# Two-layer hybrid trunk on one core: the first two weight steps multiplied unsplit

## The chip, the core and the metric

The kernel runs on one core of a Trainium2 chip. The metric is the device time of one execution in microseconds; the kernel before was timed three times, and the median is what the changed kernel is compared with.

Five engines work side by side, each through its own queue in program order: TensorE (PE: matmuls; its weight loads are listed as PEld), VectorE (DVE), ScalarE (ACT), GpSimdE (POOL) and SyncE (SP, which issues the loads). Results are handed on by semaphores.

## What is computed

A trunk of two layers over 256 tokens of width 2048, in fp32. Layer 0 is a chunked gated linear attention, layer 1 a spatial-gating MLP; each has an RMS norm ahead of it and one behind it. Cut to what matters here:

```
def reference(x, norm_pre, ..., gla_w_in, ..., sgu_w_out):
    for i in range(2):
        h = rmsnorm(x, norm_pre[i])
        y = gla_mixer(h, ...) if i == 0 else sgu_mixer(h, ...)
        x = x + rmsnorm(y, norm_post[i])
    return x

def gla_mixer(h, w_in, ...):
    proj = h @ w_in                      # (256 x 2048) @ (2048 x 6160)
    q, k, v, g, glr = jnp.split(proj, ...)
    ...
    return o @ w_out
```

The time goes into four large projections (146 MB of weights pass through once). The change concerns only the first columns of the first one: the first 512 columns of q.

## The kernel before

**Tiles.** The 256 tokens are two tiles of 128 (t = 0, 1). A projection is worked off in column groups of 512 columns, a group in eight steps (`NS`) of two K tiles of 128 rows (`KC`); one step's weights are a tile `raw` of 128 x 2 x 512, loaded by L98. Steps are numbered through the whole program: 0 to 7 are the first group, 8 to 15 the second.

**Products in three parts.** An fp32 product is made of three float32r ones. Weights are split by `split` (L105): ACT rounds `raw` to `whi` (L110), DVE or POOL takes the difference `wlo` (L111). The operand is split in the same way by `split_T` (L201): ACT writes `hTh` (L205), DVE `hTl` (L206). PE then multiplies hTh by whi, hTl by whi and hTh by wlo (L178, L179, L180). Step 0 alone is loaded and split in halves of one K tile.

**The operand of layer 0.** `make_hT(t, c)` (L280) makes four K tiles (chunk c of 4) of token tile t: four PE transposes of x (L211), a DVE multiplication by the norm's gain into `ttmp` (L284), and `split_T`. Chunk c serves steps 2c and 2c + 1, and again the same steps of all later groups of the layer.

**What sets the order.** Everything is issued in the order in which the code is run; there is no scheduler. `Stream.run` (L188) walks over the parts (step i, token tile t). In the first group two steps take turns: (0,0) (1,0) (0,1) (1,1), (2,0) (3,0) (2,1) (3,1), and so on. In the middle of a part, behind its first three products, `mid` may run a `make_hT` (L762 to L766). Behind a part, L196 fetches (loads and splits) the steps up to 2 ahead in the first group, up to 4 ahead later. With `START`, the `wlo` of steps 0, 2, 4 and 6 are POOL's; the others are DVE's. When the last step of the first group is issued, `q_done` (L295) puts the row norm on the queues: four sums of squares on ACT (`sq`, L229), two small DVE operations, one of POOL, and the scaling of the result on DVE (`q`, L301).

**The start.** Loads of x come in eight pieces of 256 KB (`load_x`), each weight step is 512 KB; L768 to L773 set their order. `WARM` transposes of the identity run on PE until the first piece of x is there, `FILL` more stand behind the first transposes of x.

Of the kernel before, what the change touches and what calls it, by code (L numbers as in the profile page):

```python
# [13 lines left out]
PSUM = bass.MemoryType.PSUM  # L14
# [10 lines left out]
AHEAD = 4  # L25
WARM = 14
FILL = 6
POOL = (1, 3, 5)
START = (0, 2, 4, 6)
SLOTS = 24  # L30
# [5 lines left out]
def trunk(  # L36
# [52 lines left out]

# [1 line left out]
    def load(parts, c, fine):  # L91
# [24 lines left out]
    class Stream:  # L116
        """Projections, column group by column group, in steps of KC K tiles; both tiles of
        tokens use a step's weights. What follows a group's products is a generator, whose
        stages come one by one between the parts that follow; a stage may ask for more parts
        before the next. Around a boundary (a group whose operand is the end of all groups  # L120
        before it) the tiles of tokens take turns of LAG steps, so that each one's products
        cover what the other waits for."""

        def __init__(self, groups, boundaries, mid):
            self.mid = mid
            self.groups = groups
            self.steps = [(g, c) for g in range(len(groups)) for c in range(NS)]
            self.raw, self.split, self.ps, self.live = {}, {}, {}, []
            n = len(self.steps)
            self.order = []  # L130
            i = 0
            turns = {b * NS + d: LAG for b in boundaries for d in (-LAG, 0)}
            turns.update({d: 2 for d in range(0, NS, 2)})
            self.pool_lo = set(START) | {b * NS + d for b in boundaries for d in POOL}
            while i < n:
                m = turns.get(i, 1)
                self.order += [(i + d, t) for t in range(NT) for d in range(m)]
                i += m

        def load(self, i):  # L140
            if i < len(self.steps) and i not in self.raw:
                g, c = self.steps[i]
                self.raw[i] = load(self.groups[g]["parts"], c, i == 0)

        def fetch(self, i):
            if i < len(self.steps) and i not in self.split:
                self.load(i)
                eng = nc.gpsimd if i in self.pool_lo else nc.vector
                self.split[i] = split(self.raw[i], eng, i == 0)

# [14 lines left out]
        def part(self, i, t):  # L165
            g, c = self.steps[i]
            grp = self.groups[g]
            w = sum(n for _, _, n in grp["parts"])
            if c == 0:
                self.ps[g, t] = acc.tile([P, 512], F32, name="acc", tag="acc")  # L170
            pt = self.ps[g, t][:, :w]
            ah, al = grp["lhs"]()
            sl = slice(t * P, (t + 1) * P)
            wh, wl = self.split[i]
            for k in range(KC):
                kt = c * KC + k
                xh, xl = ah[kt // 4][:, kt % 4, sl], al[kt // 4][:, kt % 4, sl]
                nc.tensor.matmul(pt, xh, wh[:, k, :], start=kt == 0, stop=False)  # L178
                nc.tensor.matmul(pt, xl, wh[:, k, :], start=False, stop=False)  # L179
                nc.tensor.matmul(pt, xh, wl[:, k, :], start=False, stop=kt == KT - 1)  # L180
                if k == 0 and (i, t) in self.mid:
                    self.mid[i, t]()
            if t == 0 and c == 2 and "pre" in grp:
                self.start(grp["pre"]())
            if c == NS - 1:
                self.start(grp["done"](t, pt))

        def run(self):  # L188
            freed, at = 0, 0
            for i, t in self.order:  # L190
                self.part(i, t)
                self.advance()
                if t == NT - 1:
                    freed = i + 1
                at = max(at, i)
                for j in range(at + 1, min(at + (AHEAD if at >= NS else 2), freed + SPLITS - 1) + 1):  # L196
                    self.fetch(j)
            while self.live:
                self.advance()

# [46 lines left out]

# [1 line left out]
    xs = [const.tile([P, D], F32, name=f"x{t}", tag=f"x{t}") for t in range(NT)]  # L249
# [26 lines left out]

# [281 lines left out]

# [1 line left out]
    def out_groups(key, w_out, gain, name, end, extra=None):  # L560
# [86 lines left out]

# [1 line left out]
    W2 = sgu_w_in[0]  # L649
# [110 lines left out]

# [1 line left out]
    mid = {(0, 0): lambda: make_hT(1, 0), (1, 0): lambda: make_hT(0, 1)}  # L762
    for c in range(1, 4):
        mid[2 * c - 1, 1] = lambda c=c: make_hT(1, c)
        if c < 3:
            mid[2 * c + 1, 0] = lambda c=c: make_hT(0, c + 1)  # L766
    s = Stream(groups, [layer1, len(groups)], mid)
    for c in range(4):  # L768
        load_x(0, c)
        if c < 2:  # L770
            s.load(2 * c)
            s.load(2 * c + 1)
        load_x(1, c)  # L773
    warm = aux.tile([P, 4, P], F32, name="warm", tag="aux")
# [4 lines left out]
    nc.vector.tensor_copy(gpre0, vps[:, 0:KT])  # L779
    s.fetch(0)  # L780
    make_hT(0, 0)
    for i in range(FILL):
        nc.tensor.transpose(warm[:, i % 4, :], ident, ident)
    s.fetch(1)
    s.run()
# [32 lines left out]
```

## Time and profile before

| | |
|---|---|
| median of three runs | 774.06 us (773.51 to 775.16) |
| span of the profiled execution, first to last instruction | 772.0 us |
| PE busy | 755.7 us, 98% of the span |
| DVE, ACT, POOL busy | 452.9, 353.7, 87.6 us |
| DMA | 146.28 MB, mean 189 GB/s over the span |

The profiled execution has no time of its own beside its span; the median of the timed runs is 2.06 us above the span, which is what lies around it. PE is busy nearly throughout, so the profile is read where PE is not busy or is slow: at the start, and at the boundary between the layers. The views used are the timeline (instructions in order of time, with the idle time ahead of each on its engine and what ended it), the stretches (busy time and granted TensorE clock of one microsecond each), and the chain that ended last.

### The profile page before, as it was taken

The numbers are of one execution on the slowest core, as the hardware profiler recorded it, in microseconds if no ns is written. First come the engines' busy times: TensorE is split into PE (matmuls) and PEld (weight loads), VectorE is DVE, ScalarE is ACT, GpSimd is POOL, SyncE is SP. The second block draws the span as 40 slices with busy tenths as digits, with TensorE's granted clock in tenths as the row PEclk, the third lists the DMA queues.
The fourth block names the chain that finished last, engine by engine and source line by source line (L and its number), as shares of the span: only waits on it lengthen the run. The fifth ranks groups of instructions, "written<-read, shape, count | busy, mean of one in ns | idle before, by whom it ended". The sixth has DMA issues, their size and how long they took to land.

```text
span 772.0 us, 9465 instructions
## 1 busy us (share of the span) xinstructions
PE 755.7 (98%) x3560; PEld 633.4 (82%) x3560; DVE 452.9 (59%) x521; ACT 353.7 (46%) x473; POOL 87.6 (11%) x81
## 2 busy tenths in 40 slices
PE   8999999999999999999989999999999999999995
PEld 6889998888888888888867888888888888888884
DVE  4666764645465545766588564555556565565443
ACT  4654753534354434444446454444335445344430
POOL 3210010000000001403041000132232000000000
PEclk9999999999999999999999999999999999999998
DMA  9576583465755567664724855666766455656633
GB/s 302 162 209 186 159 259 110 136 218 165 216 166 168 169 196 232 215 219 167 264 88 137 272 190 192 196 208 215 227 217 203 152 166 169 195 182 234 203 104 110
DMA packets 81318, 146.28 MB, mean 189 GB/s; under 512 B 7196, under 2 KB 14900, under 8 KB 81272
## 3 DMA queue, kind: packets, MB, share of 16 engines
q1 hardware_dynamic: 81240, 145.66, 59.5%
q8 instruction: 28, 0.46, 0.2%
q14 instruction: 18, 0.15, 0.1%
q10 hardware_dynamic: 32, 0.01, 0.0%
HBM read 143.55 MB, written 2.10 MB: 189 GB/s over the span
## 4 chain that ended last, share of the span: by engine, by line
PE 94%; DVE 2%; issue 1%; DMA 1%; ACT 0%; SPq 0%; POOLq 0%; POOL 0%; DVEq 0%; ACTq 0%
PE acc L180 30%; PE acc L178 30%; PE acc L179 30%; PE tp L211 2%; PE op L519 1%; DVE hp L614 1%; DMA raw<-in_gla_w_in_dram 1%; PE sc L440 1%; PE sp L371 0%; PE sc L433 0%; DVE h2l L206 0%; DVE wlo L111 0%; DVE x L752 0%; DVE x L590 0%; PE sc L446 0%
## 5 line engine op out<-in xcount | busy, mean ns | idle before, releaser
L111 DVE TENSOR_TENSOR wlo<-raw,whi 128x1024 fp32r<-128x1024 f32 (+2 forms) x257 | 316.6, 1254 | 119.6 <-ACT whi L110 119.2
L110 ACT CAST whi<-raw 128x1024 fp32r<-128x1024 f32 (+3 forms) x265 | 264.7, 1021 | 141.7 <-PE acc L179 57.5
L178 PE MATMUL acc<-whi,hTh 128*128 128x512 f32 (+2 forms) x416 | 158.7, 382 | 1.4 <-ACT hTh L205 1.4
L179 PE MATMUL acc<-whi,hTl 128*128 128x512 f32 (+2 forms) x416 | 155.9, 375 | 0.2 <-DVE hTl L206 0.2
L180 PE MATMUL acc<-wlo,hTh 128*128 128x512 f32 (+2 forms) x416 | 156.0, 375 | 0.0
L178 PE MATMUL acc<-whi,h2h 128*128 128x512 f32 x384 | 151.5, 394 | 0.0
L179 PE MATMUL acc<-whi,h2l 128*128 128x512 f32 x384 | 150.0, 391 | 0.0
L180 PE MATMUL acc<-wlo,h2h 128*128 128x512 f32 x384 | 149.8, 390 | 0.0
L178 PEld LDWEIGHTS acc<-whi,hTh 128*128 128x128 f32 x416 | 78.5, 189 | 13.3 <-ACT hTh L205 1.7
L180 PEld LDWEIGHTS acc<-wlo,hTh 128*128 128x128 f32 x416 | 78.4, 189 | 12.9
L179 PEld LDWEIGHTS acc<-whi,hTl 128*128 128x128 f32 x416 | 78.6, 189 | 12.7 <-DVE hTl L206 0.6
L180 PEld LDWEIGHTS acc<-wlo,h2h 128*128 128x128 f32 x384 | 72.4, 188 | 15.3
L178 PEld LDWEIGHTS acc<-whi,h2h 128*128 128x128 f32 x384 | 72.4, 189 | 14.4
L179 PEld LDWEIGHTS acc<-whi,h2l 128*128 128x128 f32 x384 | 72.4, 189 | 14.3
L178 PE MATMUL acc<-whi,ogTh 128*128 128x512 f32 x128 | 50.2, 392 | 0.0
L178 PE MATMUL acc<-whi,tTh 128*128 128x512 f32 x128 | 50.0, 391 | 0.0
L179 PE MATMUL acc<-whi,tTl 128*128 128x512 f32 x128 | 49.8, 389 | 0.0
L180 PE MATMUL acc<-wlo,ogTh 128*128 128x512 f32 x128 | 49.8, 389 | 0.0
L180 PE MATMUL acc<-wlo,tTh 128*128 128x512 f32 x128 | 49.8, 389 | 0.0
L179 PE MATMUL acc<-whi,ogTl 128*128 128x512 f32 x128 | 49.8, 389 | 0.0
L703 POOL TENSOR_TENSOR vg<-vg,gb 128x512 f32<-128x512 f32 x16 | 27.8, 1735 | 61.4 <-DVE vg L701 41.1
L229 ACT ACTIVATE sq<-acc 128x512 bf16<-128x512 f32 x16 | 9.5, 596 | 50.3 <-PE acc L180 50.3
(155 smaller groups left out, 586.9 us busy)
## 6 DMA issues: line engine op xcount, KB each, us to landing
raw<-in_sgu_w_in_dram SPq DMA_DIRECT2D x96, 512.0 KB, 4.8
raw<-in_gla_w_in_dram SPq DMA_DIRECT2D x79, 512.0 KB, 4.6
raw<-in_gla_w_out_dram SPq DMA_DIRECT2D x32, 512.0 KB, 5.7
raw<-in_sgu_w_out_dram SPq DMA_DIRECT2D x32, 512.0 KB, 4.8
raw<-in_gla_w_in_dram SPq DMA_DIRECT2D x16, 344.0 KB, 3.7
raw<-in_gla_w_in_dram SPq DMA_DIRECT2D x8, 336.0 KB, 3.6
x<-in_x_dram SPq DMA_DIRECT2D x8, 256.0 KB, 7.4
gb<-in_norm_post_dram SPq DMA_DIRECT2D x8, 256.0 KB, 6.2
```

Source lines behind the costliest of these rows:

```text
L110: nc.scalar.copy(hi[:, ks], raw[:, ks])
L111: eng.tensor_tensor(lo[:, ks], raw[:, ks], hi[:, ks].bitcast(F32), op=ALU.subtract)
L178: nc.tensor.matmul(pt, xh, wh[:, k, :], start=kt == 0, stop=False)
L179: nc.tensor.matmul(pt, xl, wh[:, k, :], start=False, stop=False)
L180: nc.tensor.matmul(pt, xh, wl[:, k, :], start=False, stop=kt == KT - 1)
L211: nc.tensor.transpose(tp[:, k, :], src[:, k * P : (k + 1) * P], ident)
L229: nc.scalar.activation(sq[:, : src.shape[1]], src, AF.Square, accum_out=dst)
L440: nc.tensor.matmul(sc[:, o + C : o + P], k2[c][:, i, o : o + P], qT[c][:, i, o + C : o + P], start=jl == 0, stop=jl == JH - 1,)
L519: nc.tensor.matmul(op, a, b, start=i == 0, stop=i == len(ops) - 1)
L614: nc.vector.scalar_tensor_tensor(hp[c], yp[c][:, t, :], r, xp[c][:, t, :], op0=ALU.mult, op1=ALU.add)
L703: nc.gpsimd.tensor_tensor(a, a, st["lng"][:, i, :], op=op)
```

## The change

Steps 0 and 1 (`WHOLE = 2`) are not split. PE multiplies `raw` itself, as fp32, by `ttmp` itself, one product in place of three; `ttmp` of chunk 0 is kept, and its `split_T`, which later groups need, is moved to the end of the first group: for t = 0 into part (7,0), for t = 1 into part (6,1). Steps 0, 1 and 2 are loaded in halves, and step 2 is split in halves. The `make_hT` of the first chunks move to other parts: (1, chunk 0) from part (0,0) to (1,0); (0, chunk 1) from (1,0) to (0,1); (1, chunk 1) from (1,1) to (2,0); the others stay. No `wlo` is POOL's in the first group. The fetch runs 1 ahead in place of 2 until part (4,0) is reached. The pieces of x come in another order among the weights. 12 transposes warm up in place of 14, 8 fill in place of 6.

```diff
-WARM = 14
-FILL = 6
+WARM = 12
+FILL = 8
-START = (0, 2, 4, 6)
+START = ()
+WHOLE = 2
...
-                self.raw[i] = load(self.groups[g]["parts"], c, i == 0)
+                self.raw[i] = load(self.groups[g]["parts"], c, i <= WHOLE)
...
                 self.load(i)
+                if i < WHOLE:
+                    return
                 eng = nc.gpsimd if i in self.pool_lo else nc.vector
-                self.split[i] = split(self.raw[i], eng, i == 0)
+                self.split[i] = split(self.raw[i], eng, i == WHOLE)
...
+                if i < WHOLE:
+                    nc.tensor.matmul(
+                        pt, self.whole[t][:, kt, :], self.raw[i][:, k, :], start=kt == 0, stop=False
+                    )
+                    if k == 0 and (i, t) in self.mid:
+                        self.mid[i, t]()
+                    continue
...
-                for j in range(at + 1, min(at + (AHEAD if at >= NS else 2), freed + SPLITS - 1) + 1):
+                ahead = AHEAD if at >= NS else 2 if at >= 2 * WHOLE else 1 if i >= WHOLE or t else 0
+                for j in range(at + 1, min(at + ahead, freed + SPLITS - 1) + 1):
...
         nc.vector.tensor_tensor(tmp, tp, gain, op=ALU.mult)
+        if c == 0:
+            s.whole[t] = tmp
+            return
         split_T(hT, t, c, tmp)
...
-    mid = {(0, 0): lambda: make_hT(1, 0), (1, 0): lambda: make_hT(0, 1)}
-    for c in range(1, 4):
+    mid = {(1, 0): lambda: make_hT(1, 0), (0, 1): lambda: make_hT(0, 1), (2, 0): lambda: make_hT(1, 1)}
+    for c in range(2, 4):
+        mid[2 * c - 1, 0] = lambda c=c: make_hT(0, c)
         mid[2 * c - 1, 1] = lambda c=c: make_hT(1, c)
...
+    mid[NS - 1, 0] = lambda: split_T(hT, 0, 0, s.whole[0])
+    mid[NS - 2, 1] = lambda: split_T(hT, 1, 0, s.whole[1])
     s = Stream(groups, [layer1, len(groups)], mid)
...
+    load_x(0, 0)
+    s.load(0)
+    s.load(1)
+    load_x(1, 0)
+    load_x(0, 1)
+    s.load(2)
+    load_x(1, 1)
+    s.load(3)
+    for c in range(2, 4):
+        for t in range(NT):
+            load_x(t, c)
```

The order on PE at the start. Before (acc_192 is the result of token tile 0, raw and whi 167 are step 0, 188 is step 1; x0 and x1 are the token tiles):

```order
L211 MATMUL tp_173<-ident_91,x0_87 128x128 x4
L783 MATMUL warm_149<-ident_91 128x128 x6
L178 MATMUL acc_192<-whi_167,hTh0_108 128x512
L179 MATMUL acc_192<-whi_167,hTl0_112 128x512
L180 MATMUL acc_192<-wlo_168,hTh0_108 128x512
L211 MATMUL tp_196<-ident_91,x1_88 128x128 x4
L178 MATMUL acc_192<-whi_167,hTh0_108 128x512
```

and with the change, up to the first product of step 3 (raw 133 and 136 are steps 0 and 1, whi 206 is step 2, whi 229 step 3; ttmp 172 and 191 are chunk 0 of the two token tiles):

```order
L223 MATMUL tp_167<-ident_91,x0_87 128x128 x4
L803 MATMUL warm_151<-ident_91 128x128 x8
L182 MATMUL acc_182<-raw_133,ttmp_172 128x512 x2
L182 MATMUL acc_182<-raw_136,ttmp_172 128x512
L223 MATMUL tp_186<-ident_91,x1_88 128x128 x4
...
L191 MATMUL acc_182<-wlo_207,hTh1_109 128x512
L223 MATMUL tp_217<-ident_91,x1_88 128x128 x4
L189 MATMUL acc_182<-whi_206,hTh1_109 128x512
L190 MATMUL acc_182<-whi_206,hTl1_113 128x512
L191 MATMUL acc_182<-wlo_207,hTh1_109 128x512
L189 MATMUL acc_182<-whi_229,hTh1_109 128x512
```

The first product waits for `ttmp` and a raw half alone; the transposes tp_217 now stand three products ahead of the first use of step 3's weights.

The order on ACT from the first cast to the fetch of step 4. Before (whi 167, 188, 208, 227 are steps 0 to 3, ttmp 220 and 246 chunk 1 of the two token tiles):

```order
L110 CAST whi_167<-raw_133 128x512 x2
L205 CAST hTh0_108<-ttmp_178 128x4x128
L110 CAST whi_188<-raw_136 128x1024
L205 CAST hTh0_108<-ttmp_201 128x4x128
L110 CAST whi_208<-raw_140 128x1024
L205 CAST hTh1_109<-ttmp_220 128x4x128
L110 CAST whi_227<-raw_142 128x1024
L205 CAST hTh1_109<-ttmp_246 128x4x128
L110 CAST whi_261<-raw_259 128x1024
```

and with the change (whi 206 is step 2, 229 step 3, 250 step 4; ttmp 201 and 222 are chunk 1 of the two token tiles):

```order
L217 CAST hTh1_109<-ttmp_201 128x4x128
L111 CAST whi_206<-raw_141 128x512 x2
L217 CAST hTh1_109<-ttmp_222 128x4x128
L111 CAST whi_229<-raw_145 128x1024
L217 CAST hTh2_110<-ttmp_241 128x4x128
L111 CAST whi_250<-raw_248 128x1024
```

The whi of step 3 stood ahead of the hTh of (token tile 1, chunk 1), and stands behind it now; so do the whi of steps 4 and 5 with the hTh of chunk 2.

The order on DVE around the end of the first group, with the change (ttmp 172 and 191 are the kept chunk 0, wlo 344 is step 8, wlo 375 step 9, r00 and q0 the row norm and the scaled result of token tile 0); before, the rows of hTl0 are not there:

```order
L112 TENSOR_TENSOR wlo_344<-raw_341,whi_343 128x1024
L218 TENSOR_TENSOR hTl0_112<-ttmp_172,hTh0_108 128x4x128
L248 TENSOR_REDUCE r00_s1_365<-r00_ss_356 128x1
L234 TENSOR_SCALAR r00_ms_367<-r00_s1_365 128x1
L316 TENSOR_SCALAR q0_355<-acc_182,r00_369 128x512
L112 TENSOR_TENSOR wlo_375<-raw_372,whi_374 128x1024
L218 TENSOR_TENSOR hTl0_112<-ttmp_191,hTh0_108 128x4x128
```

On ACT the two hTh of chunk 0 stand likewise: the first ahead of the four `sq` of token tile 0, the second behind them and behind the whi of step 9.

## Rows read from the trace of the kernel before

**Rows 1.** The page: span, and the chain that ended last, by engine.
```profile
span 772.0 us, 9465 instructions
...
PE 94%; DVE 2%; issue 1%; DMA 1%; ACT 0%; SPq 0%; POOLq 0%; POOL 0%; DVEq 0%; ACTq 0%
```

**Rows 2.** Timeline, 0 to 20 us: start, duration, instruction [idle before <-releaser].
```profile
1.42 3.25 PE L776 MATMUL warm<-ident 128*128 128x128 f32 x14 [1.42 <-POOL ident masks.py:199]
...
5.62 0.82 PE L783 MATMUL warm<-ident 128*128 128x128 f32 x6
5.82 0.69 DVE L284 TENSOR_TENSOR ttmp<-tp,gpre 128x512 f32<-128x512 f32 x1 [0.72 <-PE tp L211]
6.05 1.26 ACT L110 CAST whi<-raw 128x512 fp32r<-128x512 f32 x2 [3.52 <-DMA raw<-in_gla_w_in_dram]
...
7.86 0.70 DVE L206 TENSOR_TENSOR hTl<-ttmp,hTh 128x512 fp32r<-128x512 f32 x1 [1.35 <-ACT hTh L205]
7.88 0.49 PE L178 MATMUL acc<-whi,hTh 128*128 128x512 f32 x1 [1.45 <-ACT hTh L205]
...
8.62 0.74 PE L179 MATMUL acc<-whi,hTl 128*128 128x512 f32 x1 [0.24 <-DVE hTl L206]
...
18.32 0.39 PE L178 MATMUL acc<-whi,hTh 128*128 128x512 f32 x1
```

**Rows 3.** Stretches: busy PE, PEld, DVE, ACT, POOL (count), PEclk, DMA share, GB/s.
```profile
8.00:9.00 1.00, 0.76 (x2) 0.45 (x3) 0.57 (x1) 0.97 (x1) 1.00 (x2) 0.85 0.95 281
9.00:10.00 1.00, 1.00 (x4) 0.70 (x4) 0.89 (x1) 0.08 (x1) 0.70 (x1) 0.50 1.00 363
```

**Rows 4.** The chain in order of time: start, duration, what (near 12 and 93 us).
```profile
11.07 0.43 PE acc L179
...
12.77 0.44 PE tp L211 x4
...
13.44 0.23 PE acc L179
...
93.47 0.45 PE sp L371 x4
```

**Rows 5.** DMA issues at 4.46, 10.17 and 15.50 us: KB, us to landing.
```profile
raw<-in_gla_w_in_dram SPq DMA_DIRECT2D x1, 512.0 KB, 8.3
...
raw<-in_gla_w_in_dram SPq DMA_DIRECT2D x1, 512.0 KB, 7.3
...
raw<-in_gla_w_in_dram SPq DMA_DIRECT2D x1, 512.0 KB, 4.7
```

**Rows 6.** Timeline of ACT and DVE, 24 to 37 us.
```profile
24.18 0.62 ACT L205 CAST hTh<-ttmp 128x512 fp32r<-128x512 f32 x1 [2.23 <-DVE ttmp L284]
24.70 1.04 ACT L110 CAST whi<-raw 128x1024 fp32r<-128x1024 f32 x1
...
31.07 1.05 ACT L110 CAST whi<-raw 128x1024 fp32r<-128x1024 f32 x1
...
31.20 0.69 DVE L206 TENSOR_TENSOR hTl<-ttmp,hTh 128x512 fp32r<-128x512 f32 x1 [0.69 <-ACT hTh L205]
...
34.49 1.03 ACT L110 CAST whi<-raw 128x1024 fp32r<-128x1024 f32 x1
...
35.63 0.75 DVE L301 TENSOR_SCALAR q<-acc,r 128x512 f32<-128x512 f32 x1 [0.67 <-POOL r L224]
...
36.30 1.22 DVE L111 TENSOR_TENSOR wlo<-raw,whi 128x1024 fp32r<-128x1024 f32 x1
```

**Rows 7.** Timeline of PE at the layer boundary, its second and third wait.
```profile
398.23 1.08 PE L211 MATMUL tp<-ident,hp 128*128 128x128 f32 x4 [2.57 <-DVE hp L614]
...
409.95 0.63 PE L211 MATMUL tp<-ident,hp 128*128 128x128 f32 x4 [1.43 <-DVE hp L614]
```

**Rows 8.** Stretches behind these two waits, columns as in rows 3.
```profile
399.00:400.00 1.00, 1.00 (x5) 0.80 (x4) 0.37 (x2) 0.65 (x2) 0.00 (x0) 0.50 0.98 363
...
410.00:411.00 1.00, 1.00 (x7) 0.91 (x8) 1.00 (x3) 0.38 (x1) 0.00 (x0) 1.00 0.95 303
```

More of the change, by code (lines that the diff above doesn't have):

```diff
@@ L127, in __init__ @@
             self.steps = [(g, c) for g in range(len(groups)) for c in range(NS)]
-            self.raw, self.split, self.ps, self.live = {}, {}, {}, []
+            self.raw, self.split, self.ps, self.live, self.whole = {}, {}, {}, [], {}
             n = len(self.steps)
@@ L173, in part @@
             sl = slice(t * P, (t + 1) * P)
-            wh, wl = self.split[i]
+            wh, wl = self.split[i] if i >= WHOLE else (None, None)
             for k in range(KC):
                 kt = c * KC + k
+                if i < WHOLE:
[5 more added lines that the diff above has]
+                    continue
                 xh, xl = ah[kt // 4][:, kt % 4, sl], al[kt // 4][:, kt % 4, sl]
@@ L759, in trunk @@
     groups += out_groups("tT", sgu_w_out[0], norm_post[1], "y1", end1)
-    mid = {(0, 0): lambda: make_hT(1, 0), (1, 0): lambda: make_hT(0, 1)}
-    for c in range(1, 4):
+    mid = {(1, 0): lambda: make_hT(1, 0), (0, 1): lambda: make_hT(0, 1), (2, 0): lambda: make_hT(1, 1)}
+    for c in range(2, 4):
+        mid[2 * c - 1, 0] = lambda c=c: make_hT(0, c)
         mid[2 * c - 1, 1] = lambda c=c: make_hT(1, c)
-        if c < 3:
-            mid[2 * c + 1, 0] = lambda c=c: make_hT(0, c + 1)
+    mid[NS - 1, 0] = lambda: split_T(hT, 0, 0, s.whole[0])
+    mid[NS - 2, 1] = lambda: split_T(hT, 1, 0, s.whole[1])
     s = Stream(groups, [layer1, len(groups)], mid)
[L768 to L773, printed above, removed]
+    load_x(0, 0)
[9 more added lines that the diff above has]
+            load_x(t, c)
     warm = aux.tile([P, 4, P], F32, name="warm", tag="aux")
@@ L779, in trunk @@
     nc.vector.tensor_copy(gpre0, vps[:, 0:KT])
-    s.fetch(0)
     make_hT(0, 0)
@@ L783, in trunk @@
         nc.tensor.transpose(warm[:, i % 4, :], ident, ident)
-    s.fetch(1)
     s.run()
```

## The prediction, made blind

> **What bounds the kernel now.** I read the page first: PE ends 94% of the chain in a span of 772.0 us [rows 1]. A change in the first group moves the time by as much as it moves PE there, because behind the group PE has work without a pause up to the layer boundary, and nothing can be made up. So I read the timeline of the start next [rows 2], asking what PE waits for, then the stretches for the clock [rows 3], then the chain for the price of each kind of matmul [rows 4], and ACT and DVE at the end of the first group [rows 6], since they make what PE multiplies.
>
> The reader is to see three things. First, PE's fillers end near 6.4, and the first product starts at 7.88, after 1.45 us of idle time that ACT ends; a second wait of 0.24 us ends at 8.62 [rows 2]. Second, behind this idle time the granted clock falls to 0.50, which is 1.2 GHz in place of 2.4, near 8.7 [rows 3], and stays there for some 3.4 us: a product still takes 0.43 us at 11.07, and 0.23 us behind 12.77, where four transposes take 0.44 [rows 4]. Third, from 8.62 on nothing holds PE in this group: products follow each other, and step 3 begins at 18.32 [rows 2]. The weights of later steps are split long before PE asks for them. That slack is what the change spends.
>
> **What the change gives: an earlier start.** The first fp32 product needs only `ttmp`, which ends at 5.82 + 0.69 = 6.51, and half a raw tile, of which the first had landed at 6.05 [rows 2]. With 0.06 us of handing over (DVE to PE, 7.86 + 0.70 to 8.62 in the second wait) PE begins at 6.6 and not at 7.88, without idle time ahead: eight fillers at 0.11 each from 5.62 on end at 6.5. The two warm-up transposes that go cost nothing: what follows them waits for the first piece of x.
>
> The price of an fp32 product of 512 columns is not in the trace. Bounds: the fp32 matmuls of L371, each listed as two passes, have 130 columns and take 0.45 us for four passes, 0.112 each [rows 4]. If that goes by columns, a pass of 512 is 0.112 x 512 / 130 = 0.44; if it is set by the load of the stationary tile, a pass may cost as little as a float32r product, 0.23 [rows 4]. I take 0.43: the transposes, fp32 too with 128 columns, take 0.44 / 4 = 0.11, as L371 does. Eight products are 16 x 0.43 = 6.9 us, in place of 24 x 0.23 = 5.5. With two groups of four transposes (0.9) and some 0.2 for restarts, step 2 begins at 6.6 + 6.9 + 0.9 + 0.2 = 14.6. Step 2's six products and the four transposes that now stand in them take 6 x 0.23 + 0.44 = 1.8: PE is ready for step 3 at 16.4, and was at 18.32. **Gain 1.9 us**, the half-speed stretch of before included.
>
> The loads allow this. The weights of step 3 landed 8.3 us after their issue at 4.46, at 12.8 [rows 5]; one more piece of x ahead of them, 256 KB at 363 GB/s [rows 3], costs 0.7 us, so 13.5. The extra issues on SP are hidden, since loads wait for bytes and not for their issue. The load of step 4 waited for a split before and now waits for PE's last use of step 0, at about 12.8; it was issued at 10.17 and took 7.3 us behind the others [rows 5], so it lands at 17.5 to 18, and its split, behind the `hTh` of (0, chunk 2), does not come up before 21.
>
> **What it costs: three waits of PE**, with all later products queued behind each. The first stands at step 3. ACT's queue has the `hTh` of (1, chunk 1) ahead of step 3's `whi`, and that `hTh` waits for transposes that PE does three products before step 3. From the last transpose's start, at 15.6: result and handing over 0.3, `ttmp` 0.69, `hTh` 0.03 + 0.52 until the next operation may start, `whi` 1.05 [rows 2, 6], 0.05 to PE: ready at 18.3. PE was ready at 16.4: 1.9 us. DVE then makes `wlo` in 1.22 [rows 6] and hands over, at 19.5, while PE has two products, 0.55: another 0.7 us. Together 2.6 us. Before, this `whi` stood ahead of the `hTh`, and POOL or DVE had `wlo` done long before.
>
> Step 5 has the same pattern. Its `whi` stands behind the `hTh` of (1, chunk 2), whose transposes are done in part (3,1); but nine products lie between, 2.0 us, against the same 2.6 from transpose to `whi`. That leaves 0.5 for `whi`, or 0.8 if DVE still has step 4's `wlo` ahead of `ttmp`, and 0.7 for `wlo`: 1.2 to 1.5 us.
>
> The third is at (8,1), the first use of chunk 0 of token tile 1 in split form. Its `hTl` stands on DVE behind q0 and step 9's `wlo`, and q0 waits for the four sums of squares. In before, `whi` of step 8 starts at 31.07, `whi` of step 9 at 34.49 with the four sums between, q0 at 35.63, `wlo` of step 9 at 36.30 [rows 6]. Now one `hTh` (0.52) stands ahead of the sums. From the start of the `hTh` of (1, chunk 3): 0.52, 3.42 + 0.52, 1.14 to q0, 0.67 to `wlo`, 1.15, and `hTl` 0.69 [rows 6], 0.06 to PE: 8.2 us, and 1.0 from the last transpose to that `hTh`, 9.2 in all. PE has 34 products in this time, 34 x 0.23 + 0.1 = 7.8. Wait 1.4, with the rest of step 7's `wlo` ahead on DVE 1.7 us. The four `wlo` that POOL loses fall to DVE at 1.22 each; they lie beside products and cost only what is named here.
>
> Restarting after a wait costs 0.1 (0.49 in place of 0.39 [rows 2]), five times: 0.5 us. Sum at the full clock: -1.9 + 2.6 + 1.5 + 1.7 + 0.5, about **+4.2** after rounding.
>
> **The clock.** Behind 1.45 + 0.24 us of idle time it fell [rows 2, 3], behind 2.57 us it fell, behind 1.43 us at 409.95 it did not [rows 7, 8]. The wait at step 3 is 1.9 + 0.7 with half a microsecond of work between, so I expect a fall behind it. Such a stretch lasted 3.4 us and does half the work: 1.7 us; 0.3 of it falls into the second part of the wait, and 0.3 comes back at step 5, where a slower PE waits less. **+1.1 us.** Whether it falls again behind (8,1), at 1.7 us, lies between the two rows; if so, about +1.6 more.
>
> Sum: +5.3 us on the span of 772.0, 777.3; with the 2.06 us that lie between the span and the median, 774.06 + 5.3 = **779.4 us**.
>
> **The rivals.**
> A, no fall of the clock: 774.06 + 4.2 = 778.3; with the cheap fp32 pass another 1 us less, 777.3. (The cheap pass brings little: the waits follow the transposes and DVE's and ACT's chains.)
> B, two falls: 779.4 + 1.6 = 781.0.
> C, faster: step 3's `whi` is not held. If ACT took it when it had landed, 13.5, and step 2's casts were done, it would be there by 15.7; the start alone would be left, 774.06 - 1.9 = 772.2. It decides at PE's 16.4: any `whi` and `wlo` ready by then cost nothing. Against it: at 24.18 ACT sat idle 2.23 us for `ttmp` [rows 6], although the next weights in its queue, issued at 15.50, had landed 4.7 us later [rows 5]. The Trainium skill, page "TensorE: Matmul & The Clock Gate", the table at its head, says that the scalar engine's queue is strictly first in, first out; by that C is out, and this trace agrees with it.
> D, same: only the wait at step 3 is there, and DVE without POOL beside it (an `hTl` took 0.69 alone) keeps ahead at steps 5 and 8: -1.9 + 2.6 + 0.2 = +0.9, 775.0.
> E, the fillers do not bring the clock up. In this kernel the products would then begin at the lower level; a stretch of 3.4 us of it costs 1.7, 781. Against it: 14 transposes take 3.25 us at the start, 0.23 each, and the six fillers from 5.62 on are 0.11 apart [rows 2], before any product, so the level had come up behind transposes alone. The Trainium skill says the contrary: page "TensorE: Matmul & The Clock Gate", section "Part 4: PE-mode transpose", has it that transposes don't count as busy and the full clock doesn't engage for them. The trace disagrees here, and I go by the trace.
>
> **How the numbers follow.** Forecast (one fall) 0.60; A 0.14; B 0.10; C 0.07; D 0.05; E 0.04. The range takes A's cheap end and B, with some room for the sizes of the second and third wait: 776.6 to 781.8, leaving out C and D and a little beside them. A difference of 0.2%, 1.5 us, is about what a measurement of this kernel can tell from no change. Faster 0.07 (C), same 0.05 (D), slower 0.88.
>
> **What would show it.** In the changed kernel's trace: the first product at 6.6 and no half-speed stretch near 9; step 2 near 14.6 (13.3 if the fp32 pass is cheap); idle time of PE before step 3's L189 ended by ACT's `whi`, 1.9 us, and before its L191 ended by DVE's `wlo`, 0.7 us; the same pair at step 5; at (8,1) idle time before L190 ended by `hTl`; a stretch at 0.50 near 19 to 22. The prediction is wrong if PE passes 16 to 20 us without a wait, or if DVE and ACT are ahead of PE again by step 4.

## The result, and the profile after

The changed kernel takes **779.71 us** (median of four runs, 779.21 to 779.81), the kernel before 773.92 on the same chip: a ratio of 1.0076, 95% interval 1.0062 to 1.0090. The forecast was 779.4. The profiled execution took 779.81 us with a span of 777.7, 5.7 us longer than the span before [rows 1]. The page of after: its span, and the chain that ended last, by engine.

```profile
span 777.7 us, 9445 instructions
...
PE 92%; DVE 4%; issue 2%; ACT 1%; DMA 1%; POOL 0%; POOLq 0%; DVEq 0%; ACTq 0%
```

PE still bounds the kernel; 2% of the chain has gone over to DVE and 1% to ACT. Lines have moved: L189, L190 and L191 are the three products of a split step (L178 to L180 before), L182 is the fp32 product, L111 `whi`, L112 `wlo`, L217 `hTh`, L218 `hTl`, L241 `sq`. The timeline of PE, after: start, duration, instruction [idle before <-releaser].

```profile
4.96 1.12 PE L223 MATMUL tp<-ident,x 128*128 128x128 f32 x4 [0.50 <-DMA x<-in_x_dram]
5.87 1.92 PE L803 MATMUL warm<-ident 128*128 128x128 f32 x8
7.57 2.61 PE L182 MATMUL acc<-raw,ttmp 128*128 128x512 f32 x4
...
13.66 2.74 PE L182 MATMUL acc<-raw,ttmp 128*128 128x512 f32 x6
15.84 0.79 PE L189 MATMUL acc<-whi,hTh 128*128 128x512 f32 x1
...
19.92 0.50 PE L189 MATMUL acc<-whi,hTh 128*128 128x512 f32 x1 [1.68 <-ACT whi L111]
20.25 0.40 PE L190 MATMUL acc<-whi,hTl 128*128 128x512 f32 x1
21.18 0.50 PE L191 MATMUL acc<-wlo,hTh 128*128 128x512 f32 x1 [0.53 <-DVE wlo L112]
...
27.97 0.50 PE L189 MATMUL acc<-whi,hTh 128*128 128x512 f32 x1 [0.59 <-ACT whi L111]
...
29.23 0.50 PE L191 MATMUL acc<-wlo,hTh 128*128 128x512 f32 x1 [0.53 <-DVE wlo L112]
...
42.57 0.50 PE L190 MATMUL acc<-whi,hTl 128*128 128x512 f32 x1 [1.45 <-DVE hTl L218]
...
62.88 0.32 PE L189 MATMUL acc<-whi,hTh 128*128 128x352 f32 x1
```

The three waits stand where they were forecast: step 3 at 19.92 and 21.18, step 5 at 27.97 and 29.23, (8,1) at 42.57. The last row is the first product of 352 columns, the start of step 16; behind it PE runs as before, up to the layer boundary. The answering row of before, from its timeline of PE:

```profile
57.04 0.32 PE L178 MATMUL acc<-whi,hTh 128*128 128x352 f32 x1
```

So 62.88 - 57.04 = 5.84 us are lost before step 16, and nothing more behind it: the third wait at the boundary is shorter than in [rows 7], which gives back 0.45, and the end costs 0.3. That is the 5.7 us of the span. The boundary's third wait in the timeline of PE, after:

```profile
415.35 0.63 PE L223 MATMUL tp<-ident,hp 128*128 128x128 f32 x4 [0.78 <-DVE hp L629]
```

What held ACT and DVE, after: their timelines.

```profile
18.30 0.62 ACT L217 CAST hTh<-ttmp 128x512 fp32r<-128x512 f32 x1 [2.06 <-DVE ttmp L296]
18.83 1.04 ACT L111 CAST whi<-raw 128x1024 fp32r<-128x1024 f32 x1
...
26.35 0.62 ACT L217 CAST hTh<-ttmp 128x512 fp32r<-128x512 f32 x1 [1.89 <-DVE ttmp L296]
26.88 1.99 ACT L111 CAST whi<-raw 128x1024 fp32r<-128x1024 f32 x2
```
```profile
40.03 0.75 DVE L316 TENSOR_SCALAR q<-acc,r 128x512 f32<-128x512 f32 x1 [0.69 <-POOL r L236]
40.70 1.21 DVE L112 TENSOR_TENSOR wlo<-raw,whi 128x1024 fp32r<-128x1024 f32 x1
41.84 0.68 DVE L218 TENSOR_TENSOR hTl<-ttmp,hTh 128x512 fp32r<-128x512 f32 x1
```

ACT stands idle for 2.06 us in front of `hTh`, with step 3's `whi` behind it; `hTl` stands on DVE behind q0 and step 9's `wlo`. Two things are not as forecast. First, the start: the first product begins at 7.57 and not at 6.6, and step 2 at 15.84 and not near 14.6. The eight fillers take 1.92 us, 0.24 each, where the six of before took 0.82, 0.14 each [rows 2]: PE still ran at its lower level. The clock record of the trace has the full level from 9.03 on (5.29 before); the first two fp32 passes take 0.85 and 0.73, and 0.43 only behind them. (The column PEclk reads 1.00 there, as it does everywhere ahead of the first entry of that record; the level has to be read from the pace.) Second, behind the wait at step 3 the clock does not fall. Stretches of after, columns as in rows 3:

```profile
20.00:21.00 1.00, 0.65 (x2) 0.22 (x2) 1.00 (x1) 0.00 (x0) 0.00 (x0) 1.00 0.98 356
21.00:22.00 1.00, 0.82 (x6) 0.75 (x7) 0.12 (x1) 0.00 (x0) 0.00 (x0) 1.00 0.55 211
```

### The profile page after: what moved, and what is told of

It reads as the page before. It is cut to its first block, busy times and chain, and to the rows that moved or that the text cites. A ratio compares the mean times of both kernels' runs of the same rounds, so it can differ in the third digit from the quotient of the medians.

```text
span 777.7 us, 9445 instructions
## 1 busy us (share of the span) xinstructions
PE 758.4 (98%) x3552; PEld 631.5 (81%) x3552; DVE 452.5 (58%) x524; ACT 351.6 (45%) x471; POOL 77.3 (10%) x76
## 4 chain that ended last, share of the span: by engine, by line
PE 92%; DVE 4%; issue 2%; ACT 1%; DMA 1%; POOL 0%; POOLq 0%; DVEq 0%; ACTq 0%
PE acc L191 28%; PE acc L190 28%; PE acc L189 28%; PE tp L223 2%; DVE wlo L112 1%; PE op L534 1%; PE acc L182 1%; DVE hp L629 1%; ACT whi L111 1%; PE sc L455 1%; DMA x<-in_x_dram 1%; PE sp L386 0%; DVE ttmp L296 0%; ACT hTh L217 0%; PE sc L448 0%
## 5 line engine op out<-in xcount | busy, mean ns | idle before, releaser
L112 DVE TENSOR_TENSOR wlo<-raw,whi 128x1024 fp32r<-128x1024 f32 (+3 forms) x260 | 318.1, 1246 | 121.7 <-ACT whi L111 120.0
L111 ACT CAST whi<-raw 128x1024 fp32r<-128x1024 f32 (+3 forms) x263 | 262.4, 1021 | 139.6 <-PE acc L190 61.0
L189 PE MATMUL acc<-whi,hTh 128*128 128x512 f32 (+2 forms) x408 | 155.4, 381 | 2.3 <-ACT whi L111 2.3
L190 PE MATMUL acc<-whi,hTl 128*128 128x512 f32 (+2 forms) x408 | 152.3, 373 | 1.5 <-DVE hTl L218 1.5
L191 PE MATMUL acc<-wlo,hTh 128*128 128x512 f32 (+2 forms) x408 | 152.6, 374 | 1.1 <-DVE wlo L112 1.1
L189 PE MATMUL acc<-whi,h2h 128*128 128x512 f32 x384 | 151.5, 394 | 0.0
L190 PE MATMUL acc<-whi,h2l 128*128 128x512 f32 x384 | 150.1, 391 | 0.0
L191 PE MATMUL acc<-wlo,h2h 128*128 128x512 f32 x384 | 150.0, 391 | 0.0
L189 PEld LDWEIGHTS acc<-whi,hTh 128*128 128x128 f32 x408 | 76.7, 188 | 14.9 <-ACT whi L111 3.4
L191 PEld LDWEIGHTS acc<-wlo,hTh 128*128 128x128 f32 x408 | 76.6, 188 | 14.1 <-DVE wlo L112 2.1
L190 PEld LDWEIGHTS acc<-whi,hTl 128*128 128x128 f32 x408 | 76.7, 188 | 13.8 <-DVE hTl L218 1.9
L191 PEld LDWEIGHTS acc<-wlo,h2h 128*128 128x128 f32 x384 | 72.4, 188 | 15.3
L189 PEld LDWEIGHTS acc<-whi,h2h 128*128 128x128 f32 x384 | 72.4, 189 | 14.4
L190 PEld LDWEIGHTS acc<-whi,h2l 128*128 128x128 f32 x384 | 72.5, 189 | 14.3
L189 PE MATMUL acc<-whi,ogTh 128*128 128x512 f32 x128 | 50.2, 392 | 0.0
L189 PE MATMUL acc<-whi,tTh 128*128 128x512 f32 x128 | 50.0, 391 | 0.0
L191 PE MATMUL acc<-wlo,ogTh 128*128 128x512 f32 x128 | 49.9, 389 | 0.0
L190 PE MATMUL acc<-whi,tTl 128*128 128x512 f32 x128 | 49.8, 389 | 0.0
L191 PE MATMUL acc<-wlo,tTh 128*128 128x512 f32 x128 | 49.8, 389 | 0.0
L190 PE MATMUL acc<-whi,ogTl 128*128 128x512 f32 x128 | 49.8, 389 | 0.0
L241 ACT ACTIVATE sq<-acc 128x512 bf16<-128x512 f32 x16 | 9.5, 596 | 50.3 <-PE acc L191 50.3
```

Of the source, the lines that this page charges most:

```text
L111: nc.scalar.copy(hi[:, ks], raw[:, ks])
L112: eng.tensor_tensor(lo[:, ks], raw[:, ks], hi[:, ks].bitcast(F32), op=ALU.subtract)
L241: nc.scalar.activation(sq[:, : src.shape[1]], src, AF.Square, accum_out=dst)
```

## The experiments

All marks are read from profiled executions: the entry of the clock record at which the full level comes, the first product of step 2 on token tile 0, the first product of step 16, and the time between these two. The ratio is to the kernel before, timed beside each (773.1 to 773.9).

| kernel | us | ratio (95%) | clock up | step 2 | step 16 | between |
|---|---|---|---|---|---|---|
| before | 773.92 | 1 | 5.29 | 16.94 | 57.04 | 40.10 |
| after | 779.71 | 1.0076 (1.0062 to 1.0090) | 9.03 | 15.84 | 62.88 | 47.04 |
| warm14 | 778.93 | 1.0069 (1.0057 to 1.0082) | 6.08 | 14.52 | 62.81 | 48.29 |
| ahead2 | 777.32 | 1.0054 (1.0042 to 1.0067) | 8.56 | 15.63 | 61.24 | 45.61 |
| early_split | 778.24 | 1.0061 (1.0049 to 1.0074) | 9.60 | 16.16 | 62.21 | 46.05 |
| ahead2_early | 777.66 | 1.0052 (1.0039 to 1.0066) | 10.47 | 16.74 | 61.34 | 44.60 |
| pool46 | 778.85 | 1.0068 (1.0054 to 1.0082) | 10.71 | 16.78 | 63.53 | 46.75 |
| early_pool | 775.74 | 1.0023 (1.0013 to 1.0033) | 8.86 | 15.80 | 59.26 | 43.46 |
| all_warm14 | 773.95 | 1.0008 (1.0000 to 1.0017) | 5.26 | 14.49 | 57.93 | 43.44 |
| early_sq | 772.73 | 0.9997 (0.9988 to 1.0005) | 6.31 | 14.78 | 56.60 | 41.82 |
| early_sq16 | 772.70 | 0.9994 (0.9985 to 1.0003) | 6.15 | 14.74 | 56.56 | 41.82 |
| before_nopool | 776.61 | 1.0038 (1.0026 to 1.0050) | 4.88 | 19.08 | 60.08 | 41.00 |
| before_ahead1 | 776.19 | 1.0044 (1.0032 to 1.0057) | 4.89 | 18.97 | 61.77 | 42.80 |
| before_fill20 | 773.14 | 0.9994 (0.9985 to 1.0002) | 6.81 | 16.57 | 57.35 | 40.78 |

The last column takes out when the clock came up and leaves mainly what the splits cost. In the changed kernels two things more lie in it: four transposes, 0.44 us, which lie ahead of it before, and 0.40 us behind step 2's first product (see early_sq); in warm14 also a fall of the clock.

**warm14: is it the two warm-up transposes?**

```diff
-WARM = 12
+WARM = 14
```


> The changed kernel with 14 warm-up transposes instead of 12, nothing else. In the trace of the changed kernel PE stops at 4.46, starts again when x lands at 4.96, its first fillers are still 0.213 apart, the granted clock rises only at 9.03 (5.29 before the change), and the first product starts at 7.57, not at 6.6. Theory: the two removed transposes covered that gap, and the gap made the rise late. Then here the gap is gone, the clock rises near 5.3, the fillers end near 6.5, the first product starts near 6.6 and takes 0.43 us per pass at once; step 3's wait for whi keeps its end or ends up to 1 us earlier. Time 778.7 (1.0 less than 779.7); if PE, now earlier at step 3, waits 1 us longer there and the clock falls behind that wait, as the forecast had it, 779.7 to 780.5. Rival: the transposes had no part in it (the first fp32 products or the fillers keep the clock down): rise at 9 again, first product at 7.5, time 779.7.

The timeline of PE, and two stretches:

```profile
4.98 1.12 PE L223 MATMUL tp<-ident,x 128*128 128x128 f32 x4
5.89 1.14 PE L803 MATMUL warm<-ident 128*128 128x128 f32 x8
6.88 2.84 PE L182 MATMUL acc<-raw,ttmp 128*128 128x512 f32 x6
...
14.52 0.79 PE L189 MATMUL acc<-whi,hTh 128*128 128x512 f32 x1
...
18.60 0.51 PE L189 MATMUL acc<-whi,hTh 128*128 128x512 f32 x1 [1.68 <-ACT whi L111]
...
19.86 0.80 PE L191 MATMUL acc<-wlo,hTh 128*128 128x512 f32 x1 [0.53 <-DVE wlo L112]
...
22.59 0.63 PE L189 MATMUL acc<-whi,hTh 128*128 128x512 f32 x1
```
```profile
20.00:21.00 1.00, 1.00 (x4) 0.82 (x5) 0.00 (x0) 0.00 (x0) 0.00 (x0) 0.50 0.40 109
21.00:22.00 1.00, 1.00 (x5) 0.90 (x4) 0.46 (x1) 0.00 (x0) 0.00 (x0) 0.50 0.81 203
```

This run has about the start that the forecast took: first product at 6.88, step 2 at 14.52 (forecast 14.6). It has the same wait of 1.68 at step 3, and behind it the clock falls to 0.50. From step 3 to the next part, 22.59 - 18.60 = 3.99 us, where after takes 2.74 (22.66 - 19.92): the fall costs 1.25, the forecast had 1.1. What the two transposes give (1.32 at step 2) is gone by 22.59, and step 16 starts at 62.81 in place of 62.88. Beside its own kernel before (773.24) it takes 5.69 us more, after 5.79. The late rise and the fall stand in for each other.

**ahead2: the place of `whi` in ACT's queue.**

```diff
-ahead = AHEAD if at >= NS else 2 if at >= 2 * WHOLE else 1 if i >= WHOLE or t else 0
+ahead = AHEAD if at >= NS else 2 if i >= WHOLE or t else 0
```


> The changed kernel with the split of a step asked for two steps ahead from the first split step on, as before the change, instead of one step ahead until step 4. Theory: the waits at steps 3 and 5 (1.68 + 0.53 and 0.59 + 0.53 us in the changed kernel's trace) are there because hTh of the chunk that the same part transposes stands ahead of whi in ACT's queue. With two steps ahead whi of step 3 stands ahead of that hTh: these four waits go, PE runs into a wait for hTl or hTh of the next chunk at step 4 at most (0.2 to 0.6 us), and the wait at (8,1) for hTl stays at 1.5 or grows by up to 0.7. Time 776.9 to 778.3. Rival: whi of step 3 waits for its weights, not for its place; then the wait before L189 of step 3 stays near 1.7 and the time is 779.2 to 779.8.

The timeline of PE at (4,0) and the waits at (8,1); then DVE's `hTl` ahead of (4,0):

```profile
23.75 0.50 PE L190 MATMUL acc<-whi,hTl 128*128 128x512 f32 x1
...
38.80 0.50 PE L189 MATMUL acc<-whi,hTh 128*128 128x512 f32 x1 [0.47 <-ACT hTh L217]
...
40.89 0.50 PE L190 MATMUL acc<-whi,hTl 128*128 128x512 f32 x1 [1.59 <-DVE hTl L218]
```
```profile
23.00 0.69 DVE L218 TENSOR_TENSOR hTl<-ttmp,hTh 128x512 fp32r<-128x512 f32 x1 [0.69 <-ACT hTh L217]
```

All four waits at steps 3 and 5 are gone; between steps 2 and 16 only 1.43 us are won. The wait at (8,1) grows from 1.45 to 2.06, and a wait of 0.23 for `hTl` comes up at (6,1). Some 1.1 us more go in gaps too short to be listed: at (2,1), (4,0), (4,1) and (6,0) the first product with a new `hTl` starts 0.05 to 0.06 behind that `hTl`'s end (above: 23.00 + 0.69, then 23.75), each 0.1 to 0.3 late. The order set the waits for `whi`; PE, being earlier, waits longer for the row norm's chain and runs into `hTl`.

**early_split: the wait at (8,1).**

```diff
-mid[NS - 1, 0] = lambda: split_T(hT, 0, 0, s.whole[0])
-mid[NS - 2, 1] = lambda: split_T(hT, 1, 0, s.whole[1])
+mid[NS - 2, 0] = lambda: split_T(hT, 0, 0, s.whole[0])
+mid[NS - 1, 0] = lambda: split_T(hT, 1, 0, s.whole[1])
```


> The changed kernel with the split of chunk 0 into two parts brought forward: token tile 0 in part (6,0) instead of (7,0), token tile 1 in part (7,0) instead of (6,1). Only the second is moved behind, the first ahead of q0's work; what counts is that neither stands behind step 9's whi and wlo. Theory: the wait of 1.45 us at (8,1) is the time of hTl behind q0 and step 9's wlo on DVE; with both splits ahead of the sums of squares on ACT and ahead of q0 on DVE that wait falls to 0.0 to 0.3, and the time to 778.3 to 778.7. Rival: another late piece takes its place (step 8's or 9's wlo, for which POOL did part of the work before the change): a wait of 1 us or more for wlo at step 8 or 9, time 779.3 or more.

The timeline of PE, its one new wait:

```profile
46.21 0.50 PE L191 MATMUL acc<-wlo,hTh 128*128 128x512 f32 x1 [0.37 <-DVE wlo L112]
```

The wait at (8,1) is gone, 0.99 us are won between steps 2 and 16, and a wait of 0.37 for step 10's `wlo` comes up. The reason for the third wait holds.

**ahead2_early: both.** The edits of ahead2 and early_split together.

> Both of the two edits (splits two steps ahead; chunk 0 split in parts (6,0) and (7,0)). Theory: DVE and ACT still have more to do in the first eight steps than before (POOL makes no wlo), so the gains do not add in full: time 776.5 to 777.5, with a wait of some 0.5 to 1.5 us left somewhere between steps 4 and 9, ended by DVE. Rival: the waits were only a matter of order, and all go: 775.5 (779.7 less 3.3 of waits less 1.5, and 0.5 for the restarts).

```profile
41.92 0.50 PE L191 MATMUL acc<-wlo,hTh 128*128 128x512 f32 x1 [0.71 <-DVE wlo L112]
...
45.30 0.50 PE L191 MATMUL acc<-wlo,hTh 128*128 128x512 f32 x1 [0.33 <-DVE wlo L112]
```

Against after, 2.44 us are won between the marks. That is the sum of the two alone (1.43 + 0.99), where the expectation had less; but the waits do not all go, as the rival had it: what waits now is `wlo` at steps 9 and 10, and `hTl` at (6,1) for 0.23. The clock came up at 10.47 in the profiled execution, which takes 0.9 of the gain at step 2; the time is 0.2 above what was expected.

**pool46: order or DVE's load?** The changed kernel with `START = (4, 6)` in place of `()`.

> The changed kernel with wlo of steps 4 and 6 given back to POOL, nothing else. Two theories of the waits at steps 3 and 5. Order (mine): whi stands behind hTh in ACT's queue, with which POOL has nothing to do; the waits before L189 at steps 3 and 5 stay (1.7 and 0.5 to 1.0), those before L191 stay at 0.5, and step 9 starts no more than 1.5 us earlier than 43.84 (the wait for hTl at (8,1) shrinks); time 777.5 to 779.5. Load: DVE is simply short of time without POOL; then the waits at step 5 and (8,1) vanish, step 9 starts 3 us earlier, time 776 to 777.

```profile
20.86 0.50 PE L189 MATMUL acc<-whi,hTh 128*128 128x512 f32 x1 [1.68 <-ACT whi L111]
...
27.92 0.50 PE L191 MATMUL acc<-wlo,hTh 128*128 128x512 f32 x1 [0.49 <-POOL wlo L112]
...
43.22 0.50 PE L190 MATMUL acc<-whi,hTl 128*128 128x512 f32 x1 [1.42 <-DVE hTl L218]
```

Step 3 waits its 1.68 and (8,1) its 1.42 as before this edit. At step 4 POOL's `wlo` comes late, in place of step 5's `whi`, whose wait was expected to stay: a miss there. 0.29 us are won between the marks. Relieving DVE alone gives next to nothing, and at (8,1) its load is ruled out. At step 3 POOL has no part in either kernel; there it is ahead2, which moves no work, that shows the order.

**early_pool and all_warm14: what is left when the order is mended.** ahead2_early with `START = (4, 6)`, and the same with `WARM = 14`.

> The changed kernel with splits two steps ahead, chunk 0 split in parts (6,0) and (7,0), and wlo of steps 4 and 6 given back to POOL (POOL made those of steps 0, 2, 4 and 6 before the change). Without POOL the same kernel still waits 0.3 to 0.7 us three times for DVE near steps 6 to 10, and loses there what the order had given back; its first product of step 9 starts at 42.97 (43.84 in the changed kernel, 37.98 before). Theory: what is left of the loss behind step 3 is DVE's share of the work: two wlo of 1.2 us each go from DVE to POOL, DVE is ahead of PE again, the waits at steps 6 to 10 vanish, and step 9 starts 1.5 to 2.5 us earlier than there; time 1.0 to 2.5 us under 777.4, so 775 to 776.4. Rival: POOL, which took 2.4 us or more for one wlo before, is late itself: PE waits for POOL's wlo at step 4 or 6 and the time stays at 777 or more.

> The same with 14 warm-up transposes. With 14 in the changed kernel the clock rose at 6.08 in place of 9.03 and step 2 began at 14.52 in place of 15.84, but the clock fell behind the waits at step 3 and gave all of it back. Theory: here step 3 has no wait, so nothing lets the clock fall, and the earlier start stays: step 9 starts 1.0 to 2.2 us earlier than with 12 warm-up transposes, at 38 or before, and the time is 773.0 to 774.5, that of the kernel before. Rival: PE, being earlier, only waits longer for ACT and DVE, which follow the loads: step 9 as with 12, 775 or more.

The expectation misreads one mark: 42.97 is token tile 1 of step 9 there; token tile 0 starts at 40.59. In early_pool it starts at 38.56, 2.03 earlier, of which 0.94 is the start; in all_warm14 at 37.22. With the order mended POOL does give 1.14 between the marks (44.60 to 43.46). With 14 transposes the start is 1.31 earlier, nothing lets the clock fall at step 3, and the gain stays to step 16 (59.26 to 57.93). The waits at steps 9 and 10, which the expectation of early_pool had vanish, remain in both; in all_warm14:

```profile
38.53 0.50 PE L191 MATMUL acc<-wlo,hTh 128*128 128x512 f32 x1 [0.70 <-DVE wlo L112]
...
41.93 0.50 PE L191 MATMUL acc<-wlo,hTh 128*128 128x512 f32 x1 [0.39 <-DVE wlo L112]
```

**early_sq and early_sq16: the last two waits.** all_warm14 with the sums of squares made in front of three `split_T` that wait for `ttmp` anyway; early_sq16 with 16 warm-up transposes too.

```diff
+SQ = {(1, 1): [(0, 0)], (1, 2): [(0, 1), (0, 2), (0, 3)], (1, 3): [(1, k) for k in range(4)]}
...
+        for j, k in SQ.get((t, c), ()):
+            sumsq(xs[j][:, k * 512 : (k + 1) * 512], sss[j][:, k : k + 1])
         split_T(hT, t, c, tmp)
...
-                r0[t] = row_rstd(xs[t], f"r0{t}")
+                s1 = small(f"r0{t}_s1")
+                nc.vector.reduce_sum(s1, sss[t], axis=mybir.AxisListType.X)
+                r0[t] = rstd(s1, D, f"r0{t}")
```


> The kernel with all edits so far (splits two steps ahead, chunk 0 split in parts (6,0) and (7,0), POOL's wlo of steps 4 and 6, 14 warm-up transposes), and the sums of squares of x, which ACT made behind step 7 and for which DVE and step 9's whi and wlo waited, put into ACT's idle times in steps 2 to 5. In that kernel step 9 starts at 37.22 (37.98 before the change), but two waits for wlo of 0.70 and 0.39 us follow at steps 9 and 10, and by step 16 it is 0.9 us behind. Theory: wlo of steps 9 and 10 is late only because DVE's q0 and ACT's whi stand behind the sums; with the sums out of the way both waits go, the earlier start of 0.8 us is kept, and the time is 772.0 to 773.0 (before: 773.3). Rival: the sums now hold hTh of chunks 2 and 3 and PE waits for those at steps 4 and 6: 774 or more.

> The same with 16 warm-up transposes. In five traces with 12 the clock rose at 8.6 to 10.5, in those with 14 at 4.9 to 6.8. Theory: 16 close what is left of the gap ahead of the first transposes of x (0.52 in the kernel with 14), the rise comes at 5.5 or before in nearly all executions and the spread of the times shrinks: 771.8 to 772.8, up to 0.4 us less than with 14. Rival: the transposes of x start later, and the first product with them: 0.2 to 0.4 us more.

The timeline of PE, early_sq:

```profile
7.14 2.84 PE L183 MATMUL acc<-raw,ttmp 128*128 128x512 f32 x6
...
14.78 0.79 PE L190 MATMUL acc<-whi,hTh 128*128 128x512 f32 x1
15.41 0.40 PE L191 MATMUL acc<-whi,hTl 128*128 128x512 f32 x1
...
56.60 0.32 PE L190 MATMUL acc<-whi,hTh 128*128 128x352 f32 x1
```

No wait of PE ended by ACT or DVE is listed up to step 16, which starts 0.44 us earlier than before the change. Between the marks it still takes 1.28 us more than before (41.82 - 40.10 - 0.44). Of this, 0.40 lies behind step 2's first product, the first one behind fp32 products: the next starts 0.63 behind it (14.78 to 15.41) where later ones start 0.23 apart, in every changed kernel alike. Most of the rest are gaps too short to be listed, ahead of products with `hTl` at (2,1) and (6,1). The times, 772.73 and 772.70, are the lowest medians of all, but with ratios of 0.9997 and 0.9994 they can't be told from the kernel before. With 16 transposes the clock came up at 6.15, not at 5.5, and the median did not move; the spread of the eleven times is smaller, as expected (0.63 us against 1.27).

**before_nopool and before_ahead1: two parts of the change, each alone, in the kernel before.** `START = ()` in place of `(0, 2, 4, 6)`; and one step ahead in place of two until step 4.

```diff
-(AHEAD if at >= NS else 2)
+(AHEAD if at >= NS else 2 if at >= 4 else 1)
```


> The kernel before the change with no wlo on POOL in the first group, nothing else: the part of the change that gives DVE four more wlo, by itself. Theory: DVE's load alone costs part of the change's loss: four wlo of 1.2 us join DVE, which was busy 4.1 to 4.5 us of every 6 there, so PE waits for wlo or hTl from step 2 on: 2 to 3 us more, 775 to 776.5. Rival: the loss is a matter of order (whi and hTl behind other work) and DVE has room: 773.2 to 773.9.

> The kernel before the change with splits asked for one step ahead instead of two until step 4, nothing else: that part of the change by itself. Order theory: whi of the odd steps comes behind hTh and is late here too: waits of 0.5 to 1.7 us for whi and 0.5 for wlo at steps 2 to 5, 2 to 4 us in all, time 775.3 to 777.3. Rival: the change's waits come from the transposes of (1, chunk 1), which the change moved from part (1,1) to (2,0); where they were before, one step ahead is enough: 773.2 to 774.2.

PE in before_nopool, then in before_ahead1:

```profile
9.29 0.79 PE L178 MATMUL acc<-whi,hTh 128*128 128x512 f32 x1 [3.13 <-ACT hTh L205]
```
```profile
9.70 0.79 PE L179 MATMUL acc<-whi,hTl 128*128 128x512 f32 x1 [1.25 <-DVE hTl L206]
...
20.03 0.50 PE L180 MATMUL acc<-wlo,hTh 128*128 128x512 f32 x1 [0.44 <-POOL wlo L111]
22.07 0.50 PE L180 MATMUL acc<-wlo,hTh 128*128 128x512 f32 x1 [0.37 <-DVE wlo L111]
...
27.86 0.50 PE L180 MATMUL acc<-wlo,hTh 128*128 128x512 f32 x1 [0.49 <-POOL wlo L111]
```

Both times came out about as expected, and both in part for other reasons. Without POOL, step 0's `wlo` stands on DVE ahead of the first `ttmp`, and the first product waits 3.13 us: 2.14 of the 3.04 lost are there before step 2; between the marks only 0.90. So the other three `wlo` on DVE (steps 2, 4 and 6), where nothing else is moved, cost 0.9 us. One step ahead alone costs 2.70 between the marks, in waits for `wlo` of 0.3 to 0.5 at each of the steps 2 to 5 and none for `whi`. So the waits for `whi` in after take something beside the shorter fetch: the moved transposes of (1, chunk 1), as the rival had it, or PE's earlier arrival; no run tells these two apart. The 2.03 lost ahead of step 2 are no work of that edit, which takes effect later: see the last section. The profiled execution of before_ahead1 is the longest of its five, 778.03 with a median of 776.19.

**before_fill20: the clock's fall in the kernel before.** `FILL = 20` in place of 6.

> The kernel before the change with 20 fillers in place of 6, nothing else. It keeps PE busy from 6.44 to 7.88, where it stood idle for 1.45 us before its first product. Theory: the half-speed stretch of 3.4 us from 8.7 on comes from that idle time; without it the first products run at the full clock: up to 1.7 us less, 771.5 to 772.2 (before on this chip: 773.2), unless products then wait for splits. Rival: the stretch is there anyway, or the fillers delay the first product: 773.0 to 773.8.

Step 2 starts 0.37 earlier and step 16 0.31 later. In this execution the clock came up at 6.81, so the 20 fillers ended late and the first product began at 8.57. With the idle time filled the clock fell nowhere in the first group, as the theory had it, but a wait of 0.77 for `hTl` (see the last section) and one of 0.34 for step 10's `wlo` took what that gave. A miss in the time: the idle time was not the only thing that stood there.

## Why the prediction was right, point by point

The three waits, and so the mechanism of the loss, were right. That the number came so close (779.4 forecast, 779.71 measured) is luck: two errors cancel, and both are the clock's. The measured costs are taken from the start of one part to that of the next, against the same parts before; PE is ready for step 3 one pace (0.22) behind the start of step 2's last product, at 17.85.

| step of the forecast | forecast | measured |
|---|---|---|
| PE ready for step 3, against 18.32 | -1.9 | -0.25 (18.07) |
| step 3, two waits with restarts | +2.8 | +2.8 (1.85 + 0.91) |
| step 5, two waits with restarts | +1.4 to 1.7 | +1.6 (0.73 + 0.91) |
| (8,1), with restart | +1.5 to 1.8 | +1.75 |
| fall of the clock behind step 3 | +1.1 | 0 |
| sum at step 16 (the rest: -0.06) | +5.3 | +5.84 |
| layer boundary and end | 0 | -0.15 |

- **The start term failed**, by 1.65 us. The step is "the two warm-up transposes that go cost nothing: what follows them waits for the first piece of x". It took their time for free and left out what they do for the clock: with 12, the first product began at 7.57, 1.0 late, and the first two fp32 passes cost 0.7 more than 0.43 each. warm14 shows it: 6.88 and 14.52.
- **The sum is misadded.** Its terms as written (-1.9 + 2.6 + 1.5 + 1.7 + 0.5) make 4.4 and not 4.2, and with the lower ends of the second and third wait 3.8. With 4.4 the forecast would have been 779.6.
- **The price of the fp32 pass held.** Between 9.16 and 10.88 four passes start 0.43 apart, as taken; the cheap end (0.23) is out. The way from fp32 back to split products had no term; it costs 0.40 (early_sq).
- **The three waits held**, in place, releaser and size, and ahead2 and early_split show their causes one by one: `whi` behind `hTh`, and `hTl` behind the row norm. That it is not DVE's load is shown by pool46 for (8,1). That restarts cost 0.1 was too little: what a wait costs beyond its idle time was 0.14 to 0.38, since the trace counts idle time from the end of the last product (0.39 long, at a pace of 0.23), and the first product behind a wait is followed 0.33 to 0.34 later and not 0.23. The upper ends taken for the waits covered it.
- **The fall of the clock did not come in the forecast's place** but does come, at 1.25 us, once the start is as forecast (warm14). The same wait of 1.68 + 0.53 left the clock up in after, early_split and pool46, so it is no rule that it falls.
- **Rival E** said that fillers don't bring the clock up. In after its sign came true: the level came up only during the second fp32 pass, at a cost of 0.7 and not 1.7. Its reason did not: in warm14 eight fillers from 5.89 on take 1.14 us, and the entry at 6.08 lies ahead of the first product at 6.88. Transposes alone do bring it up. The Trainium skill, page "TensorE: Matmul & The Clock Gate", section "Part 4: PE-mode transpose", says otherwise; this trace disagrees, as that of before did.
- **C is out** by after itself: ACT stood idle 2.06 us in front of `hTh` with the next `whi` behind it. D is out: step 5 and (8,1) waited.

## What to carry to other kernels

When an edit takes a step off the front of a pipeline, write down what each in-order queue has ahead of the next step's work: here some 6 us of waits were paid for a start that was to give 1.9 and gave 0.25, because casts stood behind other casts that waited. Mending the order (two steps ahead, splits ahead of the row norm, sums in idle time, POOL's share back) took the loss between the marks from 6.5 us (47.04 - 40.10 - 0.44) to 1.3 (41.82). With 14 warm-up transposes too, the change was then ahead by 0.44 us at step 16, too little to measure in the time. Count warm-up work by what the clock does behind it, not by whether something else was waiting.

## What the runs showed of the hardware

The clock's rise hangs on little. In six traces with 12 warm-up transposes the full level came at 8.56 to 10.71 us; in seven with 14, at 4.88 to 6.81. It is not the gap behind them alone: one of 0.34 us stands ahead of the late rise in ahead2 (8.56) and one of 0.34 ahead of the early one in before_fill20 (6.81). What decides it is left open. Nor is it known how often it is late: early_pool's twelve times fall into three of 773.06 to 773.74 and nine of 775.57 to 776.54, and the trace is of one of the nine.

DVE's `hTl` waits for POOL's `wlo`. In the eight traces in which POOL makes a `wlo` of the first group, 20 `hTl` start while one runs, and each ends 0.55 to 0.56 us behind the end of that `wlo`, whether it takes 0.69 or 1.98 by then; `hTl` alone takes 0.69. `ttmp`, for which DVE reads the transposes out of PSUM, is not held: it takes 0.69 beside POOL too (13.24 in the kernel before, with POOL's `wlo` from 13.06 to 15.48).

At the start a tenth of a microsecond decides. In the kernel before, the first `hTl` took 0.70 us [rows 2]: it began at 7.86, while POOL's first half of `wlo` ran, and POOL's second half, begun at 7.98, took 1.72 and not 1.28. In before_ahead1, whose program is the same up to there, it began at 7.92, behind the second half's start, and took 1.73, so the first wait for `hTl` was 1.25 us and not 0.24, and 6.8 us of half speed followed. In before_fill20 `hTl` was held in the same way. POOL's second half and DVE in before_ahead1, then DVE in before_fill20, where POOL's second half runs from 7.94 to 9.22:

```profile
7.82 1.28 POOL L111 TENSOR_TENSOR wlo<-raw,whi 128x512 fp32r<-128x512 f32 x1
```
```profile
7.92 1.73 DVE L206 TENSOR_TENSOR hTl<-ttmp,hTh 128x512 fp32r<-128x512 f32 x1 [1.64 <-ACT hTh L205]
```
```profile
8.10 1.67 DVE L206 TENSOR_TENSOR hTl<-ttmp,hTh 128x512 fp32r<-128x512 f32 x1 [1.03 <-ACT hTh L205]
```

The Trainium skill, page "Trainium Architecture — The Big Picture", section "What this means for kernel authors", says that of all engines only DVE and GpSimd contend for SBUF, by an exclusive lock; these 20 rows fit. So what the kernel before takes ahead of step 2 differs from execution to execution (16.94 and 18.97 here) by more than the 0.44 us by which the mended kernel leads.
